# Every SBUF buffer begins on a 128-byte line, and the DMA descriptor ring shrinks from 16 KB to 1 KB a partition

## The chip, the cores and the metric

The kernel runs on one core of one Trainium2 chip. The metric is the device time of one execution in microseconds (us); lower is better. The engines are TensorE (PE, its weight loads shown apart as PEld), VectorE (DVE), ScalarE (ACT), GpSimd (POOL) and SyncE (SP), which here issues all DMAs.

## The reference

Two blocks run one after the other on 256 tokens of 1024 channels, in float32. The first has four layers with the mixers A, B, C, A; the second has two layers, each a token mixer and a feed-forward part.

```
def first_block(x, ...):
    for i in range(4):                      # A, B, C, A
        hn = rms_norm(x, norm[j])
        x = x + mixer(hn, ...)
# A: a, b, z = split(hn @ w_in); u = a * sigmoid(b); 31-tap causal convolution over tokens;
#    (silu(layer_norm(u)) * silu(z)) @ w_out
# B: q, k, v, z, f = split(hn @ w_in); 16 heads of softmax attention with a decay; (o * silu(z)) @ w_out
# C: u, b, c, z = split(hn @ w_in); 3-tap convolution; (b * conv(c * u) * silu(z)) @ w_out

def second_block(x, c, ...):
    for l in range(2):
        sh1, sc1, g1, sh2, sc2, g2 = split(silu(c) @ w_ada[l] + b_ada[l])
        y = token_mixer(x * (1 + sc1) + sh1, ...)      # attention to the 64 best keys, latent attention, gates
        x = layer_norm(ALPHA * x + g1 * y)
        y = conv_ffn(x * (1 + sc2) + sh2, ...)         # @ w_up, 3-tap convolution, silu(g) * val, @ w_down
        x = layer_norm(ALPHA * x + g2 * y)
    return x
```

What matters below: almost all of the work is products of 256 tokens with large weight matrices, each weight used once.

## The kernel before

Channels lie on the 128 partitions and tokens along them: an activation of 1024 channels is a buffer of 128 partitions x 8 chunks x 256 tokens (`x`, `hn`, `hh`, `hl`, and the five slots of the tag `big`, which hold `raw`, `rawh`, `rawl`, `U`, `C`, `Z` and others).

**Weights.** `need` loads 512 KB of weights by one DMA on SP's queue into one of five buffers `wr` (128 x 1024 float32). ACT rounds it into `wh`, and DVE (at times POOL) takes the rest, `wl = wr - wh`; both are float32r, with six slots each. Activations are split in the same way: `hh`/`hl` for a layer's input, and `ph`/`pl` (`parts`, four slots each, 128 x 256) for the input of a layer's last product.

**Products.** `mm3` makes a product of 128 x 128 weights with 256 tokens out of three float32r matmuls: `wh`·`hh`, `wh`·`hl`, `wl`·`hh` (or `ph`/`pl`). In a row of the profile `pd<-hh,wh` is such a matmul: it writes the PSUM bank `pd`, streams 256 columns of `hh` (the moving operand) and has 128 columns of `wh` loaded as weights. `tokens512` turns it round: 512 columns of `wh` or `wl` move, and 128 columns of `hh` or `rawh` are the weights. Some chunks of mixer A (`NATIVE_A`) skip the split and multiply `hn` or `raw` by `wr` in plain float32.

**Order.** `Graph` records every instruction, works out when each should run from a table of costs (`cost`, `mm`), and fixes the order on every engine before anything is issued; when TensorE has nothing to do, products of zeros (`idle`) are put in. `Graph.issue` then walks through that order. All instructions are issued by one line, so all rows of the profile carry L487; they are told apart by their names.

**Places.** `issue` makes a buffer in SBUF the first time that an instruction uses its slot:

```
if b.real is None:
    tag = b.tag if b.slot is None else f"{b.tag}{b.slot}"
    b.real = made[b.pool].tile(b.shape, b.dtype, name=b.name, tag=tag, bufs=1)
```

The pools follow one another (`const`, `weights`, `big`, `tmp`); within a pool buffers stand in the order of first use, each rounded up to a multiple of 32 bytes a partition, after a ring for DMA descriptors of 16,384 bytes. A few buffers are not a multiple of 128 bytes long (`first` 4 bytes, `cst` 3,692, `neghalf` 4, `vec` 6,752, `tb` 192, and the small `few` buffers of 32 in `tmp`), and shift everything behind them.

Of the kernel before, what the change touches and what calls it, by code (L numbers as in the profile page):

```python
# [8 lines left out]
F32 = mybir.dt.float32  # L9
F32R = mybir.dt.float32r  # L10
BF = mybir.dt.bfloat16
I32 = mybir.dt.int32
# [5 lines left out]
FIFO = 99  # L18
DEBUG = []


class Buf:
    """A tile before it has a place: what its instructions are is known, not yet when they run."""
# [8 lines left out]
class View:  # L32
    """A part of a tile: the same steps lead to it in numpy's indices and, later, in the tile's."""
# [58 lines left out]
    def region(self):  # L92
        """First and last partition, and first and last element in them."""
        a = self.arr
        off = a.__array_interface__["data"][0] - self.buf.start
        row = self.buf.row
        p, f = divmod(off, row)
        ext = sum((n - 1) * s for n, s in zip(a.shape[1:], a.strides[1:]))
        return p, p + a.shape[0], f, f + ext + 1
# [21 lines left out]
class Graph:  # L121
    """Instructions with what they need of each other, put in an order that keeps the engines busy."""

    # from the end of an instruction to the start of one that needs it
# [3 lines left out]
    # TensorE's clock doubles after a window with so much work for the array, and halves after one with so little  # L128
# [33 lines left out]
    def add(self, choices, fn, outs, ins, args, kw, key=None, group=None):  # L162
        o = Op()
        o.i, o.choices, o.fn, o.args, o.kw = len(self.ops), choices, fn, args, kw
        o.base = (self.clock + self.shift, o.i)
        o.key = (self.clock + self.shift - self.hurry, o.i)
        o.need, o.group, o.outs, o.done = set(self.extra), group, outs, False
        o.margin = self.margin
        o.hurry = self.hurry
        o.act = 0.0  # L170
        o.table = TABLE.get(args[2]) if fn == "activation" else None
        o.bufs = []
        pe = choices[0][0] == "PE"

        def meets(e, r, psum):
            # a bank counts as one, save for TensorE alone
            return psum and not (pe and e[4]) or e[0] < r[1] and r[0] < e[1] and e[2] < r[3] and r[2] < e[3]

        for w in ins:
            b, r, psum = w.buf, w.region(), w.buf.pool == "psum"  # L180
            if b not in o.bufs:
                o.bufs.append(b)
            for e in b.writes:
                if meets(e, r, psum):
                    o.need.add(e[5])
            b.reads.append(r + (pe, o.i))
        for w in outs:
            b, r, psum = w.buf, w.region(), w.buf.pool == "psum"
            if b not in o.bufs:
                o.bufs.append(b)  # L190
            for old, reads in ((b.writes, False), (b.reads, True)):
                keep = []
                for e in old:
                    if e[5] != o.i and meets(e, r, psum) and (reads or group is None or e[6] is not group):
                        o.need.add(e[5])
                        if r[0] <= e[0] and e[1] <= r[1] and r[2] <= e[2] and e[3] <= r[3]:
                            continue
                    keep.append(e)
                old[:] = keep
            b.writes.append(r + (pe, o.i, group))  # L200
        o.need.discard(o.i)
        for b in o.bufs:
            b.left += 1
        self.ops.append(o)
        return o

# [1 line left out]
    def schedule(self):  # L208
# [14 lines left out]
        # an accumulating product may begin with any of its parts: each may claim the bank  # L223
# [30 lines left out]
        def turn(t):  # L254
            """Goes on to the window of time t."""
            nonlocal tick, load, warm, after
            n = int(t / self.TICK)
            while tick < n:
                warm = load >= self.DOWN if warm else load >= self.UP
                tick, load, after = tick + 1, after, 0.0  # L260

        def room(o):
            """Whether the tiles that begin with this instruction can have their slots."""
# [13 lines left out]
        def blocked(o, e, t):  # L277
            """Whether something more urgent comes up before this would be through."""
# [153 lines left out]
    def idle_op(self, tag):  # L432
        """A product of zeros that nothing reads: it keeps TensorE's clock up while there is nothing to do."""
# [23 lines left out]
    def issue(self, tc, ctx, pools):  # L457
# [11 lines left out]
        for o in sorted(self.order, key=lambda o: o.start):  # L469
            for b in o.bufs:  # L470
                if b.real is None:
                    tag = b.tag if b.slot is None else f"{b.tag}{b.slot}"
                    b.real = made[b.pool].tile(b.shape, b.dtype, name=b.name, tag=tag, bufs=1)
# [16 lines left out]
class Engine:  # L490
    """Records an engine's instructions; their first argument, or out, is what they write."""
# [22 lines left out]
def cost(eng, fn, out, ins, args, kw):  # L514
    """The time of an instruction, about, in microseconds."""
# [64 lines left out]
def program(G, A, V):  # L580
# [90 lines left out]
    def dense(ps, half, src, kind="split", m=None):  # L671
        """One chunk of 128 outputs, channels by tokens, into half a bank."""
# [15 lines left out]
    def tokens512(srcs, m=None):  # L688
        """512 outputs, tokens by channels: a bank for each half of the tokens."""
# [15 lines left out]
    class Out:  # L705
        """1024 outputs of a product over n chunks, in four banks; the last chunks bank by bank."""
# [27 lines left out]
        def finish_chunks(self, on_chunk):  # L734
            """Chunk by chunk; what is left of the last one goes to a bank of its own, to be added to the rest."""
# [83 lines left out]
    def sums(st, i, src, grp, n):  # L819
        """Adds a chunk's sums over channels, over n, to the columns 2i, 2i+1 of st, a row for each token."""  # L820
# [4 lines left out]
    def rows(cols, n):  # L825
        """[128 tokens, n] columns, as a row for each pair of them, the same on every partition."""
# [6 lines left out]
    class Sums:  # L833
        """Means over channels, of chunks of which all but the last two are added up first."""
# [23 lines left out]
    def raw_tiles(kind):  # L858
        """Places for the next layer's input before its division by the norm, which its first products take."""
# [29 lines left out]
    def mean_rstd(st, eps):  # L889
        """From columns of means and of means of squares, the mean and 1/std of each token as rows."""  # L890
# [8 lines left out]
    def residual(out, gain=None, i0=0, late=0.0, raw="split"):  # L899
        """Adds a mixer's output to x, and takes the next layer's norm."""  # L900
# [29 lines left out]
    def modulate_all(l, after, step, late):  # L930
        """A modulation's columns, a sum over a row of weights each."""
# [20 lines left out]
    def positions():  # L952
# [9 lines left out]
        # the steps of the bias from bucket to bucket, 8 times as large, in three bfloat16 parts  # L962
# [32 lines left out]
    def bias_block(t, i0, n):  # L995
        """The bias (8 times as large) of the queries of half t and the keys 4 i0 .. 4 (i0 + n)."""
# [13 lines left out]
    def layer_a(j, raw):  # L1010
# [12 lines left out]
        def conv(c):  # L1023
            """The last taps by products on ACT and sums on Pool, then the rest on top by DVE, in PSUM."""
# [85 lines left out]
    def softmax(lt, t, p, scale, bias_of=None):  # L1110
        """Exponentials of a head's logits for 128 queries, over their sum."""
# [19 lines left out]
    def head(logits, vt, scale, p, alloc, bias_of=None):  # L1131
        """One head: logits(out, t, n) writes those of 128 queries."""
# [16 lines left out]
    def layer_b(raw):  # L1149
# [14 lines left out]
        def forget():  # L1164
# [18 lines left out]
            # rows of -c and c for every head, in three bfloat16 parts on partitions 0, 32 and 64  # L1183
# [143 lines left out]
    def residual_norm(out, l, gi, gain, shift, nxt):  # L1327
        """x = norm(x + g y), and the next product's input from it; x is kept ALPHA times as large."""
# [39 lines left out]
    def mixer(l):  # L1368
# [20 lines left out]
        # indexer queries, and the chunk of indexer keys and rope keys  # L1389
# [19 lines left out]
        # latent queries and keys  # L1409
# [24 lines left out]
        # queries of the selected attention  # L1434
# [4 lines left out]
        # scores of the keys, and the 64 best of them  # L1439
# [67 lines left out]
        # keys and values of the selected attention, and the gates, beside the attention itself  # L1507
# [170 lines left out]
def layouts(i):  # L1678
    """The inputs as the kernel reads them: transposed, permuted and repeated, never changed."""
# [132 lines left out]
```

## Time and profile before

| | |
|---|---|
| median of 3 runs | 1862.46 us (1860.3 to 1865.36) |
| profiled execution: span from first to last instruction | 1860.9 us |
| median of the runs less that span | 1.6 us |
| TensorE busy | 1792.5 us, 96% |
| VectorE, ScalarE, GpSimd busy | 81%, 60%, 23% |
| DMA | 334.91 MB, mean 180 GB/s |

The profiled execution's own time is its span; the 1.6 us by which the median of the runs lies above it are the start and end outside the span and the scatter of the runs. Matmuls overlap in the engine, so a row's own length (some 285 ns) is not what a matmul costs: that is the step from one matmul's start to the next one's.

### The profile page before, as it was taken

Reading aid. Unit: us, or ns where it says so; the run is one execution under the profiler, and the core shown is the slowest. Engines: PE = TensorE matmul, PEld = TensorE weight load, DVE = VectorE, ACT = ScalarE, POOL = GpSimd, SP = SyncE. Lnnn points to the kernel's source line nnn. Section 1 sums busy time; section 2 is a strip of 40 time slices with the busy share of each in tenths; the row PEclk is TensorE's granted clock in tenths of the full one; section 3 lists DMA queues with packets and bytes.
Section 4 is the critical chain, followed back from the end, with each engine's and each line's share of the span. In section 5 each row is a group of like instructions: output and inputs, shape, how many; then the busy total and the mean of one; then the engine's idle time right before and its main releaser. Section 6 shows DMA issues by size and latency. Waiting matters only on the chain.

```text
span 1860.9 us, 37322 instructions
## 1 busy us (share of the span) xinstructions
PE 1792.5 (96%) x14150; PEld 1718.2 (92%) x14150; DVE 1498.7 (81%) x3251; ACT 1117.2 (60%) x1985; POOL 418.8 (23%) x487
## 2 busy tenths in 40 slices
PE   9989999999999999999889999999999999999998
PEld 8878999988898989999889988999999989999998
DVE  7998989877768766679999788799887885687766
ACT  6876555544554433468766657946555568766554
POOL 4998401000011032039984100000000100000000
PEclk9999999999999999999999999999999999999999
DMA  7433557877734544543336657666876343446661
GB/s 246 136 114 136 190 188 235 254 250 257 237 117 150 181 159 159 190 150 104 123 125 202 205 176 228 218 228 207 260 253 200 137 139 123 137 136 214 189 191 54
DMA packets 107172, 334.91 MB, mean 180 GB/s; under 512 B 12784, under 2 KB 13168, under 8 KB 106992
## 3 DMA queue, kind: packets, MB, share of 16 engines
q1 hardware_dynamic: 106992, 332.52, 55.2%
q8 instruction: 111, 1.82, 0.4%
q14 instruction: 69, 0.57, 0.1%
HBM read 331.43 MB, written 1.05 MB: 179 GB/s over the span
## 4 chain that ended last, share of the span: by engine, by line
PE 54%; DVE 8%; POOL 3%; ACT 3%; DMA 3%; issue 2%; ACTq 0%; POOLq 0%; SPq 0%; DVEq 0%
PE pd L487 33%; PE po L487 17%; PE pa L487 4%; POOL C L487 3%; DMA wa<-in_w_ada 2%; DVE po L487 2%; DVE wl L487 2%; PE idle L487 1%; ACT wh L487 1%; DVE wa L487 1%; ACT tap L487 1%; DVE msk L487 1%; DVE x L487 1%; DVE IQ L487 0%; ACT L487 0%
## 5 line engine op out<-in xcount | busy, mean ns | idle before, releaser
L487 ACT ACTIVATE wh<-wr 128x1024 fp32r<-128x1024 f32 x478 | 502.7, 1057 | 435.8 <-PE pd L487 289.9
L487 PE MATMUL pd<-hh,wh 128*128 128x256 f32 x2456 | 694.9, 285 | 4.8 <-DVE up L487 1.5
L487 PE MATMUL pd<-hh,wl 128*128 128x256 f32 x2456 | 686.0, 283 | 13.2 <-DVE wl L487 13.2
L487 DVE TENSOR_TENSOR wl<-wr,wh 128x1024 fp32r<-128x1024 f32 x452 | 567.6, 1262 | 155.5 <-ACT wh L487 153.4
L487 PE MATMUL pd<-hl,wh 128*128 128x256 f32 x2456 | 686.0, 282 | 1.5 <-DVE hl L487 1.5
L487 PEld LDWEIGHTS pd<-hh,wl 128*128 128x128 f32 x2456 | 465.6, 191 | 14.3 <-DVE wl L487 13.6
L487 PEld LDWEIGHTS pd<-hh,wh 128*128 128x128 f32 x2456 | 466.3, 190 | 10.1 <-ACT up L487 2.5
L487 PEld LDWEIGHTS pd<-hl,wh 128*128 128x128 f32 x2456 | 464.7, 190 | 4.4 <-DVE hl L487 1.9
L487 POOL TENSOR_TENSOR C<-C,tap 128x233 f32<-128x233 f32 (+16 forms) x364 | 263.2, 748 | 57.8 <-ACT tap L487 48.3
L487 PE MATMUL po<-pl,wh 128*128 128x256 f32 x904 | 253.8, 284 | 2.5 <-DVE pl L487 2.5
L487 PE MATMUL po<-ph,wh 128*128 128x256 f32 x904 | 255.8, 284 | 0.3 <-DVE ph L487 0.3
L487 PE MATMUL po<-ph,wl 128*128 128x256 f32 x904 | 255.4, 283 | 0.0
L487 DVE SCALAR_TENSOR_TENSOR po<-U,vec,po 128x246 f32<-128x246 f32 (+20 forms) x532 | 214.9, 469 | 1.1
L487 ACT ACTIVATE tap<-U,vec 128x227 f32<-128x227 f32 (+17 forms) x364 | 159.7, 480 | 49.2 <-POOL C L487 29.8
L487 PE MATMUL pd<-hn,wr 128*128 128x256 f32 x768 | 179.2, 388 | 1.0 <-DVE U L487 1.0
L487 PEld LDWEIGHTS po<-pl,wh 128*128 128x128 f32 x904 | 170.6, 190 | 2.8 <-DVE pl L487 2.8
L487 PEld LDWEIGHTS po<-ph,wh 128*128 128x128 f32 x904 | 171.5, 190 | 0.8 <-PE idle L487 0.6
L487 PEld LDWEIGHTS po<-ph,wl 128*128 128x128 f32 x904 | 171.7, 190 | 0.0
L487 PEld LDWEIGHTS pd<-hn,wr 128*128 128x128 f32 x768 | 145.1, 193 | 19.7 <-DVE U L487 1.1
L487 POOL TENSOR_TENSOR r<-r,neghalf 128x4 f32<-128x4 f32 (+1 forms) x22 | 28.2, 1281 | 315.7 <-DVE r L487 217.7
L487 POOL TENSOR_TENSOR wl<-wr,wh 128x1024 fp32r<-128x1024 f32 x26 | 63.0, 2424 | 152.0 <-ACT wh L487 150.0
L487 DVE CUSTOM_DVE_ANT_0 wa<-wa,scr,mods 128x512 f32<-128x512 f32 x96 | 72.3, 753 | 27.4 <-DMA wa<-in_w_ada 26.2
(273 smaller groups left out, 2540.2 us busy)
## 6 DMA issues: line engine op xcount, KB each, us to landing
wr<-in_a_in SPq DMA_DIRECT2D x96, 512.0 KB, 3.6
wa<-in_w_ada SPq DMA_DIRECT2D x192, 256.0 KB, 3.7
wr<-in_w_up SPq DMA_DIRECT2D x88, 512.0 KB, 4.4
wr<-in_c_in SPq DMA_DIRECT2D x64, 512.0 KB, 3.6
wr<-in_m_in SPq DMA_DIRECT2D x64, 512.0 KB, 4.0
wr<-in_b_in SPq DMA_DIRECT2D x48, 512.0 KB, 4.4
wr<-in_w_dn SPq DMA_DIRECT2D x44, 512.0 KB, 4.4
wr<-in_a_out SPq DMA_DIRECT2D x32, 512.0 KB, 4.2
```

Source lines behind the costliest of these rows:

```text
L487: getattr(eng[o.eng], o.fn)(*args, **kw)
```

## The change

Line 487 of before is line 501 of the changed kernel. Comments and docstrings are gone as well, which changes no instruction. The rest of the difference is this:

```diff
+LINE = 128
+WIDTH = {F32: 4, F32R: 4, I32: 4, BF: 2}
...
+    def place(self, pool, b, tag):
+
+        size = WIDTH[b.dtype]
+        n, line = int(np.prod(b.shape[1:])), LINE // size
+        if b.pool == "psum" or n % line == 0:
+            return pool.tile(b.shape, b.dtype, name=b.name, tag=tag, bufs=1)
+        t = pool.tile([b.shape[0], -(-n // line) * line], b.dtype, name=b.name, tag=tag, bufs=1)[:, :n]
+        names = [f"a{i}" for i in range(len(b.shape) - 1)]
+        if len(names) == 1:
+            return t
+        return t.rearrange(f"p ({' '.join(names)}) -> p {' '.join(names)}", **dict(zip(names[1:], b.shape[2:])))
...
-                    b.real = made[b.pool].tile(b.shape, b.dtype, name=b.name, tag=tag, bufs=1)
+                    b.real = self.place(made[b.pool], b, tag)
...
-    nc = _bacc.Bacc("TRN2", target_bir_lowering=False, num_devices=1)
+    nc = _bacc.Bacc("TRN2", target_bir_lowering=False, num_devices=1, dynamic_dma_scratch_size=1024)
```

The buffers end at byte 228,800 of a partition before, and at 215,168 after. Where they begin, in bytes from the start of a partition, and how far into a line of 128 bytes that is:

| buffer | begins before | into a line | begins after | into a line |
|---|---|---|---|---|
| `x` | 27,936 | 32 | 12,800 | 0 |
| `hn`, `hh`, `hl` | 36,768, 44,960, 53,152 | 32 | 21,632, 29,824, 38,016 | 0 |
| `wr` (5 slots) | 79,584 and on | 96 | 64,512 and on | 0 |
| `wh`, `wl` (12 slots) | 100,064 and on | 96 | 84,992 and on | 0 |
| `wa` (2 slots) | 149,216 and on | 96 | 134,144 and on | 0 |
| `big` (5 slots: `raw`, `rawh`, `rawl`, `U`, `C`, `Z`) | 153,312 and on | 96 | 138,240 and on | 0 |
| `t2`, `t1` (4 and 8 slots; the `sq`, `tap`, `z` of rows) | from 194,272 | 96 and 64 | from 179,200 | 0 |
| `ph`, `pl` (8 slots) | 207,488 and on | 0 | 192,768 and on | 0 |
| the small `few` buffers (12 slots, 32 bytes) | from 206,560 | 0, 32, 64 or 96 | from 191,488 | 0 |

A matmul takes whole 512-byte pieces of `wh`, `wl`, `hh`, `hl` and 1,024-byte pieces of the moving operand, so that every piece begins as far into a line as its buffer does. The order of the instructions on every engine, the sizes of their operands and what they wait for are the same in both kernels, but for one row: an early VectorE memset of `tb` fills 128 x 48 words where it filled 128 x 96 halves before.

## Rows read from the trace of the kernel before

**Rows 1.** The page: the span, and the granted clock in 40 slices.

```profile
span 1860.9 us, 37322 instructions
...
PEclk9999999999999999999999999999999999999999
```

**Rows 2.** The page: the chain that ended last, shares of the span by line.

```profile
PE pd L487 33%; PE po L487 17%; PE pa L487 4%; POOL C L487 3%; DMA wa<-in_w_ada 2%; DVE po L487 2%; DVE wl L487 2%; PE idle L487 1%; ACT wh L487 1%; DVE wa L487 1%; ACT tap L487 1%; DVE msk L487 1%; DVE x L487 1%; DVE IQ L487 0%; ACT L487 0%
```

**Rows 3.** The chain in order of time: its first piece (start us, us).

```profile
508.13 1.83 PE pd L487 x16
```

**Rows 4.** Groups by line: xcount | busy us, mean ns | idle before.

```profile
L487 PE MATMUL pd<-hh,wh 128*128 128x256 f32 x2456 | 694.9, 285 | 4.8 <-DVE up L487 1.5 <-ACT hh L487 0.9 <-DVE U L487 0.7
...
L487 PE MATMUL po<-ph,wh 128*128 128x256 f32 x904 | 255.8, 284 | 0.3 <-DVE ph L487 0.3
...
L487 PE MATMUL po<-hh,wh 128*128 128x256 f32 x184 | 50.7, 276 | 0.0
...
L487 PE MATMUL pd<-wh,hh 128*128 128x512 f32 x80 | 32.1, 403 | 0.0
...
L487 PE MATMUL pd<-ph,wh 128*128 128x256 f32 x72 | 21.1, 294 | 0.4 <-ACT km L487 0.2
```

**Rows 5.** Timeline of TensorE: `hh`/`hl` moving, first and last of 89.

```profile
590.49 0.28 PE L487 MATMUL pd<-hl,wh 128*128 128x256 f32 x1
...
600.46 0.28 PE L487 MATMUL pd<-hh,wl 128*128 128x256 f32 x1
```

**Rows 6.** Timeline of TensorE: `hh`/`hl` moving elsewhere, first and last of 90.

```profile
665.19 0.28 PE L487 MATMUL pd<-hh,wh 128*128 128x256 f32 x1
...
675.67 0.28 PE L487 MATMUL pd<-hh,wl 128*128 128x256 f32 x1
```

**Rows 7.** Timeline of TensorE: `ph`/`pl` moving, first and last of 36.

```profile
999.73 0.28 PE L487 MATMUL po<-ph,wl 128*128 128x256 f32 x1
...
1003.88 0.28 PE L487 MATMUL po<-pl,wh 128*128 128x256 f32 x1
```

**Rows 8.** Timeline of TensorE: `rawh`/`rawl` moving, first and last of 10.

```profile
555.45 0.28 PE L487 MATMUL pd<-rawh,wh 128*128 128x256 f32 x1
...
556.53 0.28 PE L487 MATMUL pd<-rawh,wh 128*128 128x256 f32 x1
```

**Rows 9.** Timeline of TensorE: 512 columns of `wh`/`wl` moving, first and last of 13.

```profile
255.06 0.39 PE L487 MATMUL pd<-wh,rawl 128*128 128x512 f32 x1
...
257.78 0.39 PE L487 MATMUL pd<-wh,rawl 128*128 128x512 f32 x1
```

**Rows 10.** Timeline of TensorE: plain float32, 45 in one row.

```profile
59.73 9.88 PE L487 MATMUL pd<-hn,wr 128*128 128x256 f32 x45
```

**Rows 11.** Timeline of TensorE at half clock: first and last of 8.

```profile
943.05 0.41 PE L487 MATMUL pd<-hl,wh 128*128 128x256 f32 x1
...
944.54 0.40 PE L487 MATMUL pd<-hh,wl 128*128 128x256 f32 x1
```

**Rows 12.** Windows: length, busy PE, PEld, DVE, ACT, POOL, then PEclk, DMA share, GB/s.

```profile
943.00:944.60 1.60, 1.60 (x10) 1.60 (x9) 1.60 (x5) 0.20 (x1) 0.69 (x1) 0.50 1.00 410
1302.60:1395.70 93.10, 93.10 (x811) 93.10 (x810) 82.97 (x153) 52.33 (x78) 0.00 (x0) 1.00 0.80 257
93.00:186.10 93.10, 83.21 (x523) 76.75 (x523) 85.77 (x189) 65.65 (x142) 80.90 (x102) 0.95 0.37 125
```

**Rows 13.** ScalarE by tile: duration ns min/median/max, first and last start, forms.

```profile
L487 ACT ACTIVATE ph<-z x44: 397/399/421, 1276.8 to 1838.4; 128x256 fp32r<-128x256 f32 x44
...
L487 ACT ACTIVATE sq<-x x63: 397/417/422, 5.8 to 1848.5; 128x256 f32<-128x256 f32 x63
```

**Rows 14.** The page: DMA queues.

```profile
q1 hardware_dynamic: 106992, 332.52, 55.2%
q8 instruction: 111, 1.82, 0.4%
q14 instruction: 69, 0.57, 0.1%
```

## The prediction

> **What bounds the kernel now.** I read the chain that ended last first. It can be followed back to 508.13 us [rows 3], so it covers 1,352.8 us, and TensorE's products into `pd` and `po` make up 33% + 17% of the span on it, 930 us [rows 1, 2]. Nothing else on it has more than 4%: the kernel waits for TensorE, and for it mostly in float32r products.
>
> So the second thing to read is what one such product costs, and that is the step from start to start in TensorE's timeline, not the 285 ns in the groups [rows 4], since matmuls overlap. The reader is to see that equal products take unequal steps:
> - `hh`/`hl` moving: 9.97 us over 88 steps, 113.3 ns [rows 5]; in another place 10.48 us over 89 steps, 117.8 ns [rows 6].
> - `ph`/`pl` moving: 4.15 us over 35 steps, 118.6 ns [rows 7].
> - `rawh`/`rawl` moving: 1.08 us over 9 steps, 120.0 ns [rows 8].
> - 512 columns of `wh`/`wl` moving: 2.72 us over 12 steps, 226.7 ns [rows 9].
>
> One column a cycle at 2.4 GHz would be 106.7 ns for 256 columns and 213.3 for 512. Two rows show that the excess belongs to feeding float32r at full clock. Plain float32, which moves its columns at half that pace, takes (9.88 - 0.38) us over 44 steps, 216 ns [rows 10], where two cycles a column make 213.3. And where the granted clock is 0.50, the same `hh` products take 1.49 us over 7 steps, 213 ns [rows 11, 12], just one column a cycle at 1.2 GHz. Half the speed, no excess; full speed, 6 to 13 ns of it. Forms and sizes are equal in rows 5 to 8; what differs is where the moving buffer begins: 32, 0 and 96 bytes into a line of 128. Weights (`wh`, `wl`) begin 96 bytes in everywhere.
>
> Do lines explain the sizes? 32 float32r columns are a line's worth, 13.33 ns. A piece of 1,024 bytes that begins 96 bytes in touches nine lines, and 9 x 13.33 = 120.0; one of 2,048 bytes touches seventeen, and 17 x 13.33 = 226.7. Both are what rows 8 and 9 show. But `hh` (nine lines too) takes 113.3 or 117.8, and `ph` (eight lines, which alone would be 106.7) takes 118.6. So the place of the weights must count too: their 512 bytes touch five lines where four would do, in every product of this trace.
>
> **The change, part by part.**
>
> *Order and work.* Instructions, operands and waits are the same, so any difference comes from durations.
>
> *The ring.* The page has a hardware queue and two instruction queues [rows 14], none of descriptors written by Pool, so a smaller ring costs nothing; if Pool issued DMAs, it would matter.
>
> *Other engines.* ScalarE's `ph<-z` writes at the start of a line and takes 397 to 421 ns; `sq<-x` writes 96 bytes in and takes 397 to 422, with medians of 399 and 417 [rows 13]. The bounds are nothing and 18 ns on some 400, 4% of an engine that is idle 40% of the time and whose `wh` and `tap` have 1% of the chain each [rows 2]: 4% of 37 us is 1.5 us. I take 0. Likewise the loads: `wa` is 2% of the chain [rows 2]; were its packets a tenth shorter, that would be 4 us. I take 0 and keep 4 for the range.
>
> *TensorE.* This is the term that decides. No row shows a float32r product whose weights and moving operand both begin on a line. From below, it can't beat one column a cycle: 106.7 ns. From above, the dearest row is 120.0 [rows 8]. Nearest are the rows in which feeding doesn't limit: 2.7 ns over the ideal [rows 10] and none [rows 11]. I take 109 ns, and 216 for 512 columns, because eight lines and four are the fewest that these pieces can touch. Counting [rows 4]:
> - `hh`/`hl`: 3 x (2456 + 184) = 7,920. Over the long stretches of the timeline two steps in three are of the pace of rows 5, one of that of rows 6: 114.8 ns on average. Saved: 7,920 x 5.8 = 46 us.
> - `ph`/`pl`: 3 x (904 + 72) = 2,928, saved 2,928 x 9.6 = 28 us.
> - 512 columns: 3 x 80 and 48 of the kind in rows 9, 288 x 10.7 = 3 us.
>
> That is 77 us of TensorE's own time. Not all of it reaches the end. These products fill about 909 + 347 + 65 = 1,321 us, 71% of the span; on the chain they are (930 - 60) / 1,352.8 = 64%, with 60 us as my estimate of plain float32 among the `pd` of the chain. So 0.9 would pass at first. Where TensorE waits for others it passes less: from 93 to 186 us VectorE is busy 85.8 us of 93.1 and TensorE does 523 matmuls, against 811 in as long a stretch where it never waits [rows 12]. What is late next there is VectorE's `wl` and the convolution's sums. I take 0.75: 58 us. Sum: 1860.9 - 58 = 1803 us as a profiled span; the median of the runs lies 1.6 us above it, so 1804 us.
>
> **A rule against it.** By rows 5 to 8, 32, 0 and 96 bytes into a line give 113.3 to 120.0 ns, so the start matters. The Trainium skill (SBUF — State Buffer, Specifications (TRN2)) speaks of lines of 16 bytes in SBUF and of a penalty for crossing into a new one. All buffers before begin at multiples of 32, hence of 16, so by that rule the change gains nothing, and the time stays at 1862 us; by the rows it doesn't. The trace disagrees with the rule in so far as equal products differ by 6%.
>
> **The rivals.**
> - *Only the slow pace goes* (0.14). If feeding float32r has a floor of its own, the best step seen, 113.3 ns [rows 5], becomes that of all. For it: more than half of the steps of `hh` lie exactly there. Against: the half clock shows no floor. 7,920 x 1.5 + 2,928 x 5.3 + 1 = 28 us, x 0.75 = 21: 1841 us.
> - *Nothing changes* (0.12). The unequal steps come from when weight loads and matmuls meet, not from addresses; rows 5 and 6 have the same buffers at two paces. Against: `ph` is never at 113. 1862 us. The rule of 16-byte lines would give this too.
> - *Slower* (0.16). Weights and moving operand begin at the same place of a line afterwards, all buffers of them. The one place in the trace with equal starts is rows 8 (`rawh` and `wh`, both 96 in), and it is the dearest: two streams that go through the lines in step may get in each other's way. At 120.0 ns, 7,920 x 5.2 + 2,928 x 1.4 = 45 us; more work on the engine of the chain passes on at 0.9 or so: 1903 us. It decides once the mean step is over 116 ns. Against it: nine lines of 13.33 ns explain rows 8 without any clash, and rows 9 have the same equal starts at just their line count.
>
> **How the numbers follow.** My forecast has 0.58. With 106.7 ns for all and 0.9 passed on, the saving would be (64 + 35 + 4) x 0.9 = 93 us, 1770 us; with 111 ns and 0.7 it is (30 + 22 + 2) x 0.7 = 38 us, 1825 us. The lower end of the range is 1780, as the floor of 106.7 would leave not even the 2.7 ns of rows 10; 4 us of shorter loads lie within it. The upper end is 1866, past no change; it leaves out the slower case. A measurement here can tell 0.3%, about 6 us, from no change: faster 0.72, same 0.12, slower 0.16.
>
> **What would show it.** In the stretches of rows 5 to 7 the step should be near 109 ns at both paces' places, with 850 matmuls in 93.1 us at full clock where there are 811 [rows 12]; plain float32 and the half clock should stay at 216 and 213 ns; ScalarE's and VectorE's rows should stay within 20 ns; and TensorE's waits should grow by some 20 us, on VectorE's `wl` first. I am wrong if the step stays between 113 and 119, or if it is near 120. With the step right and the time not, the shortfall sits in waits like those between 93 and 186 us, or in more stretches at half clock, since TensorE has more time to idle [rows 1].

## The result, and the profile after

The changed kernel takes 1885.53 us (median; 1883.4 to 1889.88 over 4 runs), the kernel before beside it 1863.51 us (1860.3 to 1865.36): 1.012 times as long, 95% interval 1.01 to 1.0139. It is slower by about 22 us, where 1804 us was forecast. What came true is the rival "Slower".

The page of the profile after: the span, busy time, granted clock and the chain that ended last.

```profile
span 1881.6 us, 37322 instructions
...
PE 1821.4 (97%) x14150; PEld 1750.3 (93%) x14150; DVE 1498.1 (80%) x3251; ACT 1120.1 (60%) x1985; POOL 419.8 (22%) x487
...
PEclk9999999999999999999999999989999999999999
...
q1 hardware_dynamic: 106992, 332.52, 54.6%
...
PE pd L501 40%; PE po L501 20%; DMA wa<-in_w_ada 7%; POOL C L501 6%; PE pa L501 5%; DVE po L501 3%; DVE wl L501 2%; DVE wa L501 2%; PE idle L501 1%; ACT tap L501 1%; ACT wh L501 1%; POOL wl L501 1%; DVE msk L501 1%; DMA wr<-in_a_in 1%; DMA pi<-in_pos 0%
```

The same instructions, the same bytes, nearly the same clock (mean 0.982, before 0.984); TensorE is busy 29 us longer and still heads the chain. (Shares of the chain can't be compared with [rows 2] one by one: this chain can be followed back almost to the start, the one before only to 508.13 us.) So the step of its products is to be read. First the pieces of the chain in order of time (start us, us, what): unbroken runs of products into `pd`.

```profile
590.05 11.39 PE pd L501 x96
...
765.19 34.18 PE pd L501 x288
```

11.39 / 96 = 118.6 ns and 34.18 / 288 = 118.7, where the two paces of before were 113.3 and 117.8 [rows 5, 6]. The timeline of TensorE shows the other kinds: the first and last of 15 products with `ph`/`pl` moving, 56 plain float32 ones in one row, and the first and last of 14 at half clock.

```profile
59.69 12.33 PE L501 MATMUL pd<-hn,wr 128*128 128x256 f32 x56
...
601.28 0.28 PE L501 MATMUL po<-ph,wh 128*128 128x256 f32 x1
...
602.95 0.28 PE L501 MATMUL po<-ph,wl 128*128 128x256 f32 x1
...
1061.29 0.41 PE L501 MATMUL pd<-hl,wh 128*128 128x256 f32 x1
...
1064.07 0.41 PE L501 MATMUL pd<-hh,wl 128*128 128x256 f32 x1
```

`ph`: 1.67 us over 14 steps, 119.3 ns (118.6 before [rows 7]). Plain float32: (12.33 - 0.39, a product's own length) / 55 = 217 ns (216 [rows 10]). Half clock: 2.78 / 13 = 213.8 ns (213 [rows 11]). Three windows (length, busy PE, PEld, DVE, ACT, POOL with counts, then PEclk, DMA share, GB/s) answer to [rows 12]:

```profile
1061.30:1064.00 2.70, 2.70 (x14) 2.70 (x14) 0.00 (x0) 0.00 (x0) 1.65 (x1) 0.50 1.02 391
...
93.00:186.10 93.10, 83.45 (x510) 76.92 (x510) 87.54 (x192) 64.74 (x141) 79.84 (x103) 0.93 0.36 122
1302.60:1395.70 93.10, 93.10 (x784) 93.10 (x783) 80.69 (x150) 51.13 (x76) 0.00 (x0) 1.00 0.80 250
```

Where TensorE never waits it does 784 matmuls in 93.1 us, not 811. Only float32r at full clock has become dearer. Over all steps under 150 ns between two such products, `hh`/`hl` moving went from 115.2 to 118.8 ns on average, `ph`/`pl` from 118.2 to 119.7. Times their counts, `hh` makes 28.5 us of the loss and `ph` 4.4.

Adding up TensorE's steps by kind gives the whole difference of the spans: float32r products at full pace 1,266.8 to 1,299.3 us (+32.5), plain float32 164.6 to 163.0, the other matmuls 170.3 to 167.5, `idle` products 51.4 to 51.6, and all longer steps (over 150 ns for a float32r product of 256 columns), which are waits and half clock, 202.6 to 195.1. Together that is +20.8 us, where the spans differ by 20.7. About a third of what the products lost was made up in the longer steps and the small products.

### The profile page after: what moved, and what is told of

It reads as the page before. It is cut to its first block, busy times and chain, and to the rows that moved or that the text cites. A ratio compares the mean times of both kernels' runs of the same rounds, so it can differ in the third digit from the quotient of the medians.

```text
span 1881.6 us, 37322 instructions
## 1 busy us (share of the span) xinstructions
PE 1821.4 (97%) x14150; PEld 1750.3 (93%) x14150; DVE 1498.1 (80%) x3251; ACT 1120.1 (60%) x1985; POOL 419.8 (22%) x487
## 4 chain that ended last, share of the span: by engine, by line
PE 66%; DVE 11%; DMA 8%; POOL 8%; issue 4%; ACT 3%; SPq 0%; POOLq 0%; ACTq 0%; DVEq 0%
PE pd L501 40%; PE po L501 20%; DMA wa<-in_w_ada 7%; POOL C L501 6%; PE pa L501 5%; DVE po L501 3%; DVE wl L501 2%; DVE wa L501 2%; PE idle L501 1%; ACT tap L501 1%; ACT wh L501 1%; POOL wl L501 1%; DVE msk L501 1%; DMA wr<-in_a_in 1%; DMA pi<-in_pos 0%
## 5 line engine op out<-in xcount | busy, mean ns | idle before, releaser
L501 PE MATMUL pd<-hh,wl 128*128 128x256 f32 x2456 | 694.3, 286 | 14.3 <-DVE wl L501 14.3
L501 PE MATMUL pd<-hh,wh 128*128 128x256 f32 x2456 | 702.3, 288 | 5.9 <-DVE U L501 2.3
L501 PE MATMUL pd<-hl,wh 128*128 128x256 f32 x2456 | 694.5, 286 | 1.5 <-DVE hl L501 1.5
L501 PEld LDWEIGHTS po<-pl,wh 128*128 128x128 f32 x904 | 173.4, 193 | 2.7 <-DVE pl L501 2.6
L501 DVE CUSTOM_DVE_ANT_0 wa<-wa,scr,vec 128x512 f32<-128x512 f32 x96 | 71.9, 749 | 28.3 <-DMA wa<-in_w_ada 27.9
```

The source lines that it names most:

```text
L501: getattr(eng[o.eng], o.fn)(*args, **kw)
```

## The experiments

What could be behind a dearer step? Three theories:

- *Pairs of starts.* The step depends on where weights and moving operand begin, both together; the change made that pair worse.
- *Lines.* Being on a line of 128 bytes is itself what costs, whatever the other operand does.
- *The ring.* Something outside the operands, with the smaller ring.

A notation for what follows: starts are the addresses in a partition that the compiled programs give, modulo 256; d is the moving operand's less the weights', modulo 256. Steps are also given in cycles of 2.4 GHz: 113.3 ns is 272, 117.7 is 282.5, 118.75 is 285 and 120.0 is 288. Before, `hh` had 160 against weights at 224 (d = 192), `ph` 128 (d = 160), `raw` 224 (d = 0). After, weights are at 0, `hh` at 128 (d = 128), `ph` and `raw` at 0 (d = 0).

**The ring alone** (on before):

```diff
-    nc = _bacc.Bacc("TRN2", target_bir_lowering=False, num_devices=1)
+    nc = _bacc.Bacc("TRN2", target_bir_lowering=False, num_devices=1, dynamic_dma_scratch_size=1024)
```

> The kernel before with the smaller descriptor ring alone: every buffer moves down by 15,360 bytes, which is 60 times 256, and keeps its place within lines of 32 to 256 bytes. Theory 1 (the places of weights and moving operand within a line, against each other, set the step): steps of hh stay at 113.3 and 117.8 ns, of ph near 118.6, the time within 0.3% of 1863 us. Theory 2 (the ring itself, or where buffers lie in the whole of SBUF, made the change slow): 1875 to 1886 us.

1863.76 us against 1864.78: ratio 1.0002, interval 0.9981 to 1.0024 (10 runs). All buffers moved down by 15,360 bytes, a multiple of 256, and the paces stayed (115.5 and 117.8 ns on average). The theory of the ring falls.

**A map of starts.** The kernel loads `x`, and then does only runs of 24 products (`wh`·`hh`, `wh`·`hl`, `wl`·`hh`), three times for each of 8 x 8 starts (`PHASES` are 0 to 224 in steps of 32 bytes), with `idle` products between runs:

```diff
+    for dw in PHASES:
+        for dm in PHASES:
...
+                for k in range(8):
+                    m = slice(k * S + dm // 4, (k + 1) * S + dm // 4)
+                    w = slice(k * 128 + dw // 4, (k + 1) * 128 + dw // 4)
+                    mm(ps[:, 0], wh[:, w], hh[:, m], 0.12, grp)
+                    mm(ps[:, 0], wh[:, w], hl[:, m], 0.12, grp)
+                    mm(ps[:, 0], wl[:, w], hh[:, m], 0.12, grp)
```

> Leaves out the whole computation: only float32r products of the kernel's pattern (wh.hh, wh.hl, wl.hh; 24 in a row, three times each with a few bfloat16 products between), for 8 x 8 starts of the weights and of the moving operand, 0 to 224 bytes past the buffers' beginning in steps of 32; all four buffers begin at the same place of a line of 256 bytes. Theory 1 (what counts is the difference of the two starts): the step depends on the difference alone; equal starts give 120.0 ns, a moving operand 64 bytes behind the weights 113 to 118 ns. Theory 2 (what counts is how many lines each piece touches): the step is lowest where both begin on a line of 128, whatever the difference. Theory 3 (only the moment at which weight load and matmul meet counts): the three repeats of one pair differ as much as the pairs do, 113 to 120 ns everywhere.

Its timeline of TensorE, of two cases: equal starts (both at 0), and weights at 64 with the moving operand at 0.

```profile
338.67 0.28 PE L487 MATMUL pd<-hh,wl 128*128 128x256 f32 x1
...
340.35 0.28 PE L487 MATMUL pd<-hl,wh 128*128 128x256 f32 x1
...
486.02 0.28 PE L487 MATMUL pd<-hh,wh 128*128 128x256 f32 x1
...
487.95 0.28 PE L487 MATMUL pd<-hh,wl 128*128 128x256 f32 x1
```

1.68 us over 14 steps, 120.0 ns; and 1.93 over 17, 113.5. The mean step of the later products of each run, in cycles, worked out from these starts (rows: weights; columns: moving operand; three runs each; in the row of 128 most runs follow one another without a break, and one figure stands for the three):

```
        0            32           64           96           128          160          192          224
  0   288/288/288  280/281/280  283/283/283  288/288/288  285/288/288  285/282/285  283/272/283  284/284/284
 32   285/284/285  288/288/288  279/281/279  283/283/283  288/288/288  285/285/284  285/285/281  283/272/272
 64   272/272/272  284/284/285  288/288/288  283/280/281  283/283/283  288/288/288  285/284/285  282/288/281
 96   282/282/282  283/283/283  284/284/284  288/288/288  279/279/281  283/283/283  288/288/288  288/288/285
128   285          282          283          284/284/285  288          283          283          288
160   288/288/288  285/285/284  285/285/282  283/272/283  284/285/284  288/288/288  280/279/283  283/283/283
192   283/272/283  287/287/288  285/285/288  285/285/288  283/283/272  284/284/284  287/288/288  280/280/280
224   279/279/280  283/283/283  288/288/288  287/288/285  288/282/284  283/283/272  284/284/284  288/287/288
```

The diagonals say it: equal starts cost 288 whether they are on a line (0, 128) or not, and in this map 272 is seen only at d = 192, where it changes with 283. That agrees with the kernel before (rows 5 and 6 are d = 192: 272 and 282.5) and after (d = 128 and 0: 285 and 288).

**The difference, in the kernel, off the lines.** On before, an unused tile ahead of a pool's first buffer moves the whole pool of weights (`wr`, `wh`, `wl`, `wa`) by 192 bytes, so that `wh` and `wl` begin at 160, where `hh` begins; `raw` gets 64 bytes more so that `big` and `tmp` stay where they were modulo 256. Nothing that counted lies on a line now, save `ph`, which did before.

```diff
+PADS = {'wr': 192, 'raw': 64}
...
+                    if b.name in pads:
+                        n = pads.pop(b.name)
+                        made[b.pool].tile([128, n // 4], F32, name="pad_" + b.name, tag="pad_" + b.name, bufs=1)
```

> The kernel before with the weights moved alone, so that they begin 160 bytes past a line of 256, as hh and hl do; no buffer is put on a line of 128. Theory 1 (the difference of the two starts, modulo 256, sets the step): hh and hl now have the same start as their weights, so their step rises from 113.3 and 117.8 to 119 to 120 ns, ph (32 bytes behind the weights) stays near 118; 7,900 products by 4 to 5 ns, 0.9 of it at the end: 1890 to 1900 us. Theory 2 (beginning on a line of 128 is what made the change slow): the time stays at 1863 us.

1888.35 us against 1864.15: 1.0122, interval 1.0082 to 1.0162. The chain in order of time, and the window in which TensorE never waits:

```profile
594.05 11.50 PE pd L492 x96
...
768.56 34.55 PE pd L492 x288
```

```profile
1302.60:1395.70 93.10, 93.10 (x783) 93.10 (x782) 80.71 (x155) 51.51 (x77) 0.00 (x0) 1.00 0.79 251
```

11.50 / 96 = 119.8 ns, 34.55 / 288 = 120.0, and 783 matmuls. One move of the weights, from one place off a line to another, makes as large a slowdown as the whole change. The theory of lines falls.

**The good difference, in the changed kernel.** The same pads, now on the changed kernel, keep all lengths padded, but put the weights at 64 and the moving operands at 0 (d = 192):

```diff
+PADS = {'hn': 128, 'wr': 192, 'raw': 192}
```

> The changed kernel with three pads: every buffer that moves in a float32r product begins at a multiple of 256, the weights 64 bytes past one. Theory 1: the step of all products with 256 columns of hh, hl, ph, pl, rawh or rawl is 113.3 ns, as in the map at this pair; against the kernel before 7,900 x 1.5 to 2 and 2,900 x 5 ns less, 0.8 of it at the end: 1835 to 1848 us. Theory 2 (a start on a line of 128 is slow): about 1885 us, as the changed kernel. Rival: hh keeps a second pace of 117.8 ns, 1850 to 1860 us.

1858.9 us against 1864.15: 0.9966, interval 0.9941 to 0.9992 (12 runs). So the loss is undone by the pads, but the hoped 1835 to 1848 are missed:

```profile
589.53 11.31 PE pd L506 x96
...
761.83 32.64 PE pd L506 x288
```

Pieces at 11.31 / 96 = 117.8 and 32.64 / 288 = 113.3 ns: both paces live on. Of all 10,108 steps of `hh` and `ph`, 6,497 are of 112 to 114 ns and 3,283 of 117 to 119. The map had 272 in all three runs for this pair; most likely that was chance, for the next map has 272 in three of six and in one of six runs at the same difference.

**`ph` alone**, on before: 32 bytes ahead of the first `ph` give it d = 192 too.

```diff
+PADS = {'ph': 32}
```

> The kernel before with ph and pl moved by 32 bytes alone, to 64 bytes behind the weights modulo 256, as hh and hl are. Theory 1: the step of ph and pl falls from 118.2 to between 113.3 and 117.8 ns, 115 on average, 2,900 x 3 ns, 0.8 of it at the end: 1853 to 1859 us. Theory 2: no change, 1863 us.

1860.92 us against 1864.15: 0.9974, interval 0.9952 to 0.9996 (12 runs). The step of `ph` falls from 118.2 to 115.7 ns, half at 272 and half at 282.5; that of `hh`, whose starts are as before, is 115.5 instead of 115.2. 2,928 x 2.5 = 7.3 us less on `ph`, 2 more on `hh`, and 3.2 measured.

**A finer map.** Weights fixed at 128, the moving operand in steps of 16 bytes over 512, six runs each, and `wh` 64 bytes apart from `wl`:

```diff
-PHASES = range(0, 256, 32)
+CASES = [(0, 0, m) for m in range(0, 512, 16)] + [(64, 0, 0), (0, 64, 0)]
```

> Leaves out the whole computation, as the first map: the weights stay at one start, the moving operand begins 0 to 496 bytes behind it in steps of 16, six repeats each; then two cases in which wh and wl begin 64 bytes apart. Theory 1: the pattern repeats after 256 bytes, with 120.0 ns at 0 and 256 and the lowest steps at 192 and 448; 16 bytes off a multiple of 32 it lies between its neighbours. Rival: some start in steps of 16 goes below 113.3 ns. With wh and wl apart, the step follows the weights that are loaded while the product runs, the next product's, not its own.

The pattern comes back after 256 bytes. At d = 192 three of six runs are at 272 and three at 282.6; 256 bytes further on it is one and five. At d = 112 all six runs settle at 272 within some ten products (274.9 on average with the approach), and nothing lies below 272. That a start 16 bytes off a multiple of 32 lies between its neighbours was wrong: d = 112 lies far below 96 and 128 (287 and 284 cycles or more). With `wh` and `wl` 64 apart, so that one has d = 192 and the other d = 0, all three kinds of product run at 117 to 119 ns: a product's price can't be told from its own weights alone here.

**d = 112 in the kernel, by moving the weights** (on after, weights at 144, the rest at 0):

```diff
+PADS = {'hn': 128, 'wr': 128}
...
+        if b.tag in ("wh", "wl"):
+            return pool.tile([128, 1088], b.dtype, name=b.name, tag=tag, bufs=1)[:, 36:1060]
```

> The changed kernel with wh and wl begun 144 bytes past a multiple of 256 and all that moves in a float32r product of 256 columns at a multiple of 256: the moving operand begins 112 bytes after its weights, modulo 256, where all six repeats of the second map fell to 113.3 ns within about ten products and stayed there. Theory 1 (the difference sets the step, and which paces can last): nearly all steps of hh and ph at 113.3 ns, mean below 114.5; 7,900 x 1.3 and 2,900 x 4.2 ns less than before, 0.8 of it at the end: 1842 to 1852 us. Rival: other work breaks the pace too often, mean 115 as with a difference of -64: 1855 to 1860 us.

1887.1 us against 1864.78: 1.0136, interval 1.0107 to 1.0164. A clear miss: the long piece of its chain shows 120.0 ns.

```profile
768.17 34.56 PE pd L508 x288
```

So the difference alone isn't the law. In the map the weights lay at a multiple of 32 and the moving operand at an odd multiple of 16; in this kernel it is the other way round.

**Sizes.** Weights of 128, 64 and 32 columns, with 256, 384 and 512 moving columns:

```diff
+CASES = [(c, n, m) for c in (128, 64, 32) for n in (256, 384, 512) for m in (0, 64, 112, 128, 192)]
```

> Leaves out the whole computation: products with 128, 64 or 32 columns of weights and 256, 384 or 512 moving columns, at differences of 0, 64, 112, 128 and 192 bytes, four repeats each. Theory A (each weight load takes a fixed time from the moving stream): the excess over one column a cycle is the same for 256, 384 and 512 columns at one difference, 13.3 ns at 0, and halves with 64 columns of weights. Theory B (feeding float32r has a floor of 17 cycles for 16 columns): the excess grows with the columns, 6.7 ns at 256 and 13.3 at 512, and stays when the weights shrink.

Cycles above one a column, the lowest and highest of the cases that settled: with 128 weight columns 16 to 32 at 256 moving, 32 to 40 at 384, 32 to 48 at 512; with 64 weight columns 16 to 32, 31 to 40, 32 to 47; with 32 columns 16 to 27, 24 to 40, 34 to 53. (The first run of d = 0 is left out: for much of it the granted clock is 0.50.) The lowest figures, 16 at 256 and 32 at 512, are one cycle in 16 columns; 384 has 32 as a rule, 24 at the lowest, which is that rate as well. That is theory B's floor, but not the whole price: at one pair of starts the excess need not grow with the columns. With equal starts and 128 weight columns, the case of [rows 8, 9], it is 32 cycles at 256, at 384 and at 512 (up to 37 in one run), as theory A had it. First and last of 18, 18 and 9 such products:

```profile
18.75 0.28 PE L487 MATMUL pd<-hh,wh 128*128 128x256 f32 x1
...
20.79 0.28 PE L487 MATMUL pd<-hh,wl 128*128 128x256 f32 x1
...
60.55 0.33 PE L487 MATMUL pd<-hh,wh 128*128 128x384 f32 x1
...
63.50 0.34 PE L487 MATMUL pd<-hh,wl 128*128 128x384 f32 x1
...
127.91 0.39 PE L487 MATMUL pd<-hh,wh 128*128 128x512 f32 x1
...
129.72 0.39 PE L487 MATMUL pd<-hh,wl 128*128 128x512 f32 x1
```

2.04 / 17 = 120.0 ns, 2.95 / 17 = 173.5 and 1.81 / 8 = 226: 288, 416 and 543 cycles. With 64 weight columns it falls to 16 at 256, which is half, but is 40 at 512. So neither theory holds for all cases.

**Starts in steps of 4 bytes**, weights at 128:

```diff
+CASES = [(0, 0, m) for m in range(0, 256, 4)]
```

> Leaves out the whole computation, as the second map: differences of 0 to 252 bytes in steps of 4, four repeats each. Theory 1: 288 cycles (120.0 ns) at 0; 272 (113.3 ns) near 112 and, in some repeats, 192; between them 279 to 288. Rival: some difference that no buffer of the kernels has had goes below 272 cycles.

No case below 272. d = 112 gives 274.7 to 274.9 in all four runs, 64 and 192 give 272 or 282.6. Starts off the multiples of 16 give 281 to 299, those on them 272 to 289.

**d = 112 by moving the other operand** (on after, weights at 128, `hh`, `hl`, `ph`, `pl` at 240):

```diff
+PADS = {'wr': 128}
...
+        if b.tag in ("c_hh", "c_hl", "ph", "pl"):
+            t = pool.tile([128, n + 64], b.dtype, name=b.name, tag=tag, bufs=1)[:, 28:28 + n]
+            return t if len(b.shape) == 2 else t.rearrange("p (a b) -> p a b", b=b.shape[2])
```

> The changed kernel with the weights 128 bytes past a multiple of 256 and hh, hl, ph, pl 240 past one: the same difference of 112 bytes as in the last kernel, but with the very starts of the second map, whose weights began on a line of 128. Theory 1a (the starts themselves count, not the difference alone; weights off a multiple of 32 are dear): steps as in the map, 113.3 ns lasting, mean below 114.5, 1840 to 1852 us. Theory 1b (the difference of 112 is dear outside the map, since accumulating products with other work beside them never reach the lasting pace): steps of 118 to 120 ns, 1880 to 1890 us.

1851.6 us against 1867.04: 0.9923, interval 0.9897 to 0.995. 

```profile
588.49 10.88 PE pd L509 x96
...
757.74 32.64 PE pd L509 x288
```

10.88 / 96 and 32.64 / 288 are both 113.3 ns. Same d as the kernel at 1887.1 us: which of the two operands is off the multiples of 32 makes 2%.

**Starts of the weights.** d of 0, 112 and 192, each with weights at 128 to 240 in steps of 16, six runs each:

```diff
+CASES = [(w, w, w + d) for d in (0, 112, 192) for w in range(0, 128, 16)]
```

> Leaves out the whole computation: weights begin 0 to 112 bytes past a line in steps of 16, the moving operand 0, 112 or 192 bytes after them, six repeats each. Theory 1 (difference alone): all eight rows of one difference are alike, 288, 272 to 276 and 272 or 282.5 cycles. Theory 1a: they are alike only for weights at multiples of 32, and dearer at the odd multiples of 16.

Mean step in cycles from the seventh product of a run on, six runs a case (the very first run, mostly at a granted clock of 0.50, is left out):

| weights begin at | d = 0 | d = 112 | d = 192 |
|---|---|---|---|
| 128, 160, 192, 224 | 286 to 288 | 272 to 278 | 272 or 283 |
| 144, 176, 208, 240 | 280 to 284 | 283 to 288 | 272 to 274, in the end 272 in all 24 |

Its timeline for weights at 144, first d = 112 (173.4 to 176.1 us), then d = 192:

```profile
174.53 0.28 PE L487 MATMUL pd<-hh,wh 128*128 128x256 f32 x1
...
176.07 0.28 PE L487 MATMUL pd<-hl,wh 128*128 128x256 f32 x1
...
321.10 0.28 PE L487 MATMUL pd<-hl,wh 128*128 128x256 f32 x1
...
322.91 0.28 PE L487 MATMUL pd<-hh,wl 128*128 128x256 f32 x1
```

1.54 us over 13 steps, 118.5 ns; 1.81 over 16, 113.1. Moving both operands by 16 bytes, so that the weights begin at an odd multiple of 16, turns d = 112 from good to bad, and takes the second pace from d = 192. It fits the miss at weights 144. Since at one difference both starts move together, this map doesn't say which of the two counts: in all three columns the better row is the one in which the moving operand begins at an odd multiple of 16.

**The pair that the map names** (on after, weights at 144, moving operands at 80, d = 192):

```diff
+PADS = {'hn': 128, 'wr': 128}
...
+        if b.tag in ("wh", "wl"):
+            return pool.tile([128, 1088], b.dtype, name=b.name, tag=tag, bufs=1)[:, 36:1060]
+        if b.tag in ("c_hh", "c_hl", "ph", "pl", "big"):
+            n = int(np.prod(b.shape[1:]))
+            t = pool.tile([128, n + 64], b.dtype, name=b.name, tag=tag, bufs=1)[:, 20:20 + n]
+            return t if len(b.shape) == 2 else t.rearrange("p (a b) -> p a b", b=b.shape[2])
```

> The changed kernel with the weights 144 bytes past a multiple of 256 and all that moves in a product of 256 columns 80 past one: the pair of starts at which all six repeats of the last map ran at 113.3 ns from the first products on. No operand of these products begins on a line of 128, or at a multiple of 32. Theory 1a (the pair of starts sets the step): mean below 114, 10,000 products by 0.5 ns less than with the last kernel and 2 less than before, 0.8 of it at the end: 1842 to 1850 us. Rival: in the kernel the pace is broken as it was with a difference of -64 on multiples of 32, mean 115: 1855 to 1860 us.

1846.56 us against 1864.93: 0.9897, interval 0.9872 to 0.9922 (6 runs). It beats both kernels, and none of its products' operands begins on a line of 128 bytes, or even on a multiple of 32.

```profile
592.50 10.88 PE pd L512 x96
...
761.53 32.64 PE pd L512 x288
```

```profile
1302.60:1395.70 93.10, 93.10 (x823) 93.10 (x823) 83.50 (x156) 53.75 (x81) 0.00 (x0) 1.00 0.82 259
```

All products of these two pieces go at 113.3 ns, the mean over the kernel is 113.8, and 823 matmuls fit where before had 811 and after 784.

**All kernels together.** Mean steps (under 150 ns, as above); TensorE's products are 7,920 x the change of `hh` + 2,928 x that of `ph` against before (115.2, 118.2); the time is the difference of the medians of the runs. The steps come from one execution of each kernel, and executions of one kernel differ by up to 24 us, so the two columns agree only roughly.

| kernel | weights, `hh`, `ph` begin at | `hh` ns | `ph` ns | products, us | time, us |
|---|---|---|---|---|---|
| changed | 0, 128, 0 | 118.8 | 119.7 | +33 | +22.0 |
| weights alone | 160, 160, 128 | 119.7 | 118.3 | +36 | +24.2 |
| d = 112 by the weights | 144, 0, 0 | 119.4 | 119.3 | +36 | +22.3 |
| ring alone | 224, 160, 128 | 115.5 | 117.8 | +1 | -1.0 |
| `ph` alone | 224, 160, 160 | 115.5 | 115.7 | -5 | -3.2 |
| d = 192 | 64, 0, 0 | 114.9 | 115.0 | -12 | -5.3 |
| d = 112 by the moving side | 128, 240, 240 | 114.2 | 114.0 | -20 | -15.4 |
| the pair | 144, 80, 80 | 113.8 | 113.8 | -24 | -18.4 |

Time follows the products in all of them but the ring alone, where both differences are too small to tell; 0.45 to 0.8 is passed on. That is what settles the cause: the change is slower because it moved weights and moving operands to a worse pair of starts, and no other part of it shows in the time.

## Why the prediction was wrong, step by step

- *What bounds the kernel*: right. The time follows the float32r step, and in the sum of TensorE's steps nothing else grew by more than 0.2 us.
- *That starts matter, not only moments*: right, and shown: moving only the weights by 192 bytes makes 24 us. The rival "Nothing changes" falls with it. But starts are not all: with the same starts, d = 192 has two lasting paces, as [rows 5, 6] had suggested.
- *The ring, the other engines*: right. 1.0002 for the ring; and by tile, ScalarE's rows after (duration ns min/median/max) against [rows 13]:

```profile
L501 ACT ACTIVATE ph<-z x44: 397/398/421, 1284.3 to 1858.9; 128x256 fp32r<-128x256 f32 x44
...
L501 ACT ACTIVATE sq<-x x63: 400/419/423, 5.7 to 1869.2; 128x256 f32<-128x256 f32 x63
```

  `sq` begins on a line now, and its median went from 417 to 419: the 18 ns between it and `ph` had nothing to do with lines.
- *The price at starts 0 and 0*: this is the step that failed. "I take 109 ns, and 216 for 512 columns, because eight lines and four are the fewest that these pieces can touch." Measured: 118.8 ns for `hh` and 119.7 for `ph`, and for 512 columns 228 on average where `rawh` or `rawl` is the weights and 232 where `hh` or `hl` is (228 and 230 before). Counting touched lines fitted two rows of the trace by chance (9 x 13.33 = 120.0 and 17 x 13.33 = 226.7): both have equal starts, and the map of sizes gives equal starts 32 cycles above one a column at either length, on a line too. At starts 0/0 a piece touches eight lines and takes 120.0 all the same. The prediction named [rows 8], equal starts at the dearest step, in its rival, with "It decides once the mean step is over 116 ns", and set it aside for the count of lines. It was the row nearest to the new state of `ph`.
- *No floor, because the half clock shows none*: the floor of 113.3 ns was refused by [rows 11]. No settled run of 256 columns in the five maps lies below 272 cycles. The rival "Only the slow pace goes" had the floor right, and the pair 144/80 shows what it described: it was priced 21 us under before, and the pair gains 18.4.
- *What passes to the end*: 0.75 was taken for a gain, 0.9 for a loss. The changed kernel passed 22.0 / 33 = 0.67, the pair 18.4 / 24 = 0.77. The rival "Slower" had the direction right and 1903 us too high, because of the 0.9 and because it took 120.0 for all. Its mechanism, equal starts, holds for `ph` alone: modulo 256, after which the pattern comes back, `hh` begins 128 bytes from its weights, and that pair's 285 to 288 cycles (118.8 ns on average in the kernel) make most of the loss.
- *The rule of 16-byte lines* of the Trainium skill (SBUF — State Buffer, Specifications (TRN2)) was weighed and not followed. Both kernels' buffers begin at multiples of 16, so by it nothing would change; the time changed by 1.2%. The map in steps of 4 bytes agrees with it in so far as starts off the multiples of 16 are mostly dearer (up to 299 cycles against at most 289), and disagrees in that multiples of 16 differ among themselves by 16 cycles (272 and 288).

What is still open: why 272 is the floor, why moving both operands by 16 bytes exchanges good and bad differences and which of the two makes it, and what decides between the two paces at d = 192. The runs give prices for pairs of starts, not the mechanism that makes them.

## What to carry to other kernels

Aligning every buffer to the same boundary also makes their starts equal, and for two operands of one product that can be among the dearest pairs; maps of the step over pairs of starts pointed to the cause in one run and to a faster kernel in a few. Where no row shows the new state, the row that shares most with it (here equal starts, at the dearest step) is better evidence than a formula that fits two rows and fails the third. And of a saving or loss per product on the busiest engine, 0.45 to 0.8 reached the end in this kernel.

## What the runs showed of the hardware

- A float32r product of 128 x 128 weights and 256 columns takes 113.3 to some 120 ns at a granted clock of 1.00, by the starts of its two operands modulo 256 (up to 124.6 ns at starts off the multiples of 16); in the kernels this was worth 1846.6 to 1888.4 us. Plain float32 (216 to 217 ns) and the half clock (213 to 214 ns) were the same before and after.
- Two lasting paces, 272 and 282.5 cycles, with the same starts: a run of products keeps the one that it falls into (d = 192). At d = 112 (weights at a multiple of 32) products fall into 272 within some ten steps; with equal starts there they stay at 288.
- The difference of the starts is not all: with the weights at odd multiples of 16, d = 192 goes at 272 in all 24 runs, and d = 112 at 283 to 288; with the weights at multiples of 32 it is 272 or 283, and 272 to 278.
- The cycles above one a column are at least 16 at 256 moving columns, with 128, 64 or 32 columns of weights alike, and at least 32 to 34 at 512. At equal starts with 128 weight columns they are 32 at 256, 384 and 512 alike.
